# Common start addresses, and four small moves, in a transformer block with a dense mixture of 16,384 experts

## The chip, the cores and the metric

The kernel runs on one core of a Trainium2 chip. The metric is the device time of one execution in microseconds. Its engines are named as in the profile: PE (TensorE, matrix products), DVE (VectorE), ACT (ScalarE), POOL (GpSimd) and SP (SyncE, which only issues DMAs here). Each engine works through its own list of instructions in order and waits for other engines and for DMAs by semaphores. PEld is PE's load of the weight operand, which overlaps its products.

## The reference

One layer over 512 frames and 16 meta tokens of 2048 features, in float32. Two attentions share one input projection; a gate weighs each branch; then a mixture of single-neuron experts (PEER) is added.

```python
hn = _rmsnorm(h, norm_mix_g[l])
proj = hn @ w_in[l]
c_q, c_kv, k_rope, q_sb, k_sb, v_sb, gate_a, gate_b = jnp.split(proj, split_at, axis=-1)
...
y_a = _mla_attention(q_nope, q_rope, k_nope, k_rope, v_a, chunk_id).reshape(b, lp, A_WIDTH)
y_b = _stick_breaking_attention(...).reshape(b, lp, B_WIDTH)
merged = (jax.nn.sigmoid(gate_a) * (y_a @ w_branch_a[l])
          + jax.nn.sigmoid(gate_b) * (y_b @ w_branch_b[l]))
h = h + merged @ w_out[l]
h = h + _peer(_rmsnorm(h, norm_ffn_g[l]), peer_w_q[l], peer_sub_keys[l], peer_u[l], peer_v[l])
...
def block(xb):                       # in _peer, for 128 tokens
    q = (xb @ w_q).reshape(PEER_BLOCK, PEER_HEADS, 2, PEER_HALF)
    s = jnp.einsum('thcd,hcnd->thcn', q, sub_keys).astype(jnp.float32)
    s1, i1 = lax.top_k(s[:, :, 0], PEER_TOPK)
    s2, i2 = lax.top_k(s[:, :, 1], PEER_TOPK)
    ...
    g = jax.nn.softmax(top_s, axis=-1).reshape(PEER_BLOCK, -1)
    h = jnp.einsum('tkd,td->tk', u[idx], xb)
    act = (g * jax.nn.gelu(h.astype(jnp.float32), approximate=False)).astype(xb.dtype)
    return jnp.einsum('tk,tkd->td', act, v[idx])
```

## The kernel before

**Products in three parts.** Each float32 operand is split into a high part that PE's fast float32 form holds exactly and the remainder: `hi = round(x)`, `lo = x - hi`. `mm3` (L256) then makes three products for every pair of operands: lo weights by hi input (L257), hi by lo (L258), hi by hi (L259). A weight tile of 128x1024 is loaded by SP into `wr` (L239, from `front`, `ut` or `vb`), ACT writes its high part `wh` (L245), DVE the remainder `wl` (L246). `wh` and `wl` come from a ring of three buffers in the pool `weights`; in the v stage every fourth comes from a pool of its own, `weights_v`, and in the u stage two of five from the upper part of `hgh` and `hgl` (`Tail`, then named hgh and hgl as weights too).

**Stages,** by start in the profile. From 0: the input projections (`proj`, L340) with the moving input `xh`, `xl`, in pieces of 512 columns (frames) or of two times 264 (frames and meta tokens), and stick-breaking attention between them. From 815: multi-head latent attention, whose outputs lie in `yah`, `yal`. From 974: the branch products with `yh_b`, `yl_b` and `yah`, `yal`, whose gated sum is split into `mgh`, `mgl`. From 1154: the output projection with `mgh`, `mgl`. From 1332: the expert queries (16 blocks `hc` with `hgh`, `hgl`, 512 columns) and their scores, from which the top 16 keys are ranked. From 1549: u. For 336 of the 512 tokens all 16,384 experts are computed, as dense products of 336 columns, in 128 groups e of 128 experts with two weight tiles each; the other 176 tokens fetch the rows of their chosen experts by indirect DMAs on POOL (`row`) and multiply them on DVE (L1257). From 2536: v, with `vah`, `val` as the input (activations times gates of 4 groups, 336 columns each), 32 steps of 8 weight tiles; rows of v are added up on DVE into `xg` (L1265), dense sums into `acc` (L1443).

**Order.** A tile scheduler orders each engine's instructions by dependences and its own estimate of costs, not by their place in the text. A dependence added by hand (`follows`, L1286) makes an instruction stand behind the last `wl` split on DVE without any semaphore.

**The places that the change touches.**
- Start addresses. The pools of the left side lie behind the constants, a tile of 337 float32 columns per partition, which holds the two selection tables `sel_b` and `sel_c` too; pools of the right side are placed from the other end. `pad_y` (L817) is a tile that nothing uses.
- Copied norms. `rh_` holds each token's norm. For the 48 tokens handled in the groups of rows `BC`, DVE copies norms into `rr` (shown as tile sc, L1076), PE transposes them (L1074, L1077) and DVE copies the results out to `rcol` and `rcolb` (L1078, L1080). This stands at block `hc == 1`.
- Gates. Routing (`routing`, L1186) turns ranked keys into gates; `gates_of` (L1126) then spreads them over the 16,384 experts: DVE makes one-hot tiles of a pair of tokens (L1144), ACT scales them into `wos` (L1161, three buffers), PE multiplies (L1155) three steps later in the text. In the u stage `beside` runs one gate step per half of a group and one routing step per half at first, and three of four from e = 20.
- Gate weights `wt` are a tile of their own; `gw_all` holds the gates of each token and is stored by SP (L930) for the rows' tokens.
- Residual addition. In steps 3 to 14 of the v stage the residual of one of the 12 first feature blocks is loaded into the one buffer `hres` at tile 0 of the step and added to `acc` (L1421) at tile 6.

Of the kernel before, what the change touches and what calls it, by code (L numbers as in the profile page):

```python
# [23 lines left out]
P = 128  # L24
# [44 lines left out]
def _constants():  # L69
# [11 lines left out]
        "sel_b": (p[:, None] * NS[1] // P == np.arange(NS[1])[None, :]),  # L81
        "sel_c": (p[:, None] * NS[2] // P == np.arange(NS[2])[None, :]),
        "eps": np.full((P, 1), EPS),
        "halfpi": np.full((P, 1), math.pi / 2),
# [16 lines left out]
for _i in range(4):  # L101
    MLA_MASK[_i, META + P * _i + 64:META + P * (_i + 1)] = NEG
    MLA_MASK[_i, LEN + P * _i:LEN + P * _i + 64] = 1.0
GAINS = {"mix": (0, 16), "q": (16, 20), "kv": (20, 24), "ffn": (24, 40), "fin": (40, 56)}
# [26 lines left out]
def _layout(x, positions, meta_tokens, norm_mix_g, w_in, mla_q_norm_g, mla_w_uq, mla_kv_norm_g,  # L131
# [50 lines left out]
    for i, n in enumerate(FRONT):  # L182
# [10 lines left out]
            "pos": c(pos[None]), "gains": c(gains), "mla_mask": MLA_MASK, "const": CONST_ARR[0], "const_m": CONST_ARR[1], "const_e": CONST_ARR[2],  # L193
# [22 lines left out]
def body(tc, nc, a, dbg=None):  # L216
# [399 lines left out]
    yal = yp.tile([P, H, SEQ], F32R, name="yal")  # L616
    stage = ExitStack()
# [199 lines left out]
    sp2.tile([P, 16], F32, name="pad_y")  # L817
# [108 lines left out]
    def spread_rows():  # L926
        b0 = ND - (NT - 1) * P

        SP.dma_start(eob_d, er[b0:])
        SP.dma_start(gwb_d, gw_all[b0:, NT - 1])  # L930
        for o, t0, n in ((0, NS[2], NS[1]), (NS[1], 0, NS[2])):
            for to, src in ((eob, eob_d), (gwb, gwb_d)):
                SP.dma_start(to[:, o:o + n], src[t0:t0 + n].rearrange("t (r k) -> (t r) k", r=P // n))
# [4 lines left out]
    def route(ti, n, pool):  # L938
# [57 lines left out]
        if ti == NT - 1:  # L996
            V.tensor_copy(er, ev)

# [13 lines left out]
    with tc.tile_pool(name="score", bufs=2, side="left") as sp_, \  # L1012
# [28 lines left out]
        for hc in range(16):  # L1041
# [28 lines left out]
            if hc == 1:  # L1070
                pt_ = ps_tile()
                rr = sp_.tile([P, 4, NK], F32, name="sc")
                V.memset(rh_[:, :ND], 1.0)
# [44 lines left out]
    wos = up.tile([P, 3, 2, P, 2], F16, name="wos", bufs=1)  # L1118
    piece = up.tile([P, P], F16, name="piece", bufs=1)
    wt = up.tile([P, 2, P], F32, name="wt", bufs=1)  # L1120
# [5 lines left out]
    def gates_of(ti):  # L1126
# [8 lines left out]
        V.tensor_copy(wt[:, 0], piece)  # L1135
        V.scalar_tensor_tensor(rest, w, GW, wt[:, 0], ALU.mult, ALU.subtract)
        V.tensor_copy(piece, rest)
        V.tensor_copy(wt[:, 1], piece)
# [3 lines left out]
        for p in range(m + 4):  # L1142
            if p < m:
                V.tensor_tensor(ohs[p % 4], keys_b[:, :, None, 2 * p:2 * p + 2].to_broadcast([P, 2, P, 2]),  # L1144
                                iota_b[:, None].to_broadcast([P, 2, P, 2]), ALU.is_equal)
            yield
            gate_out()
            q0 = p - 3
            if q0 >= 0 and q0 % 2 == 0 and q0 < m:
                bank = ps_tile()  # L1150
                for q in range(q0, min(q0 + 2, m)):
                    for t in range(2):
                        o = ((q - q0) * 2 + t) * P
                        for c in (1, 0):
                            T.matmul(bank[:, o:o + P], ohs[q % 4][:, 1, :, t], wos[:, q % 3, c, :, t],  # L1155
                                     start=c == 1, stop=c == 0)
                banks.append((bank, ti * P + 2 * q0, min(4, n - 2 * q0)))
            if p < m:
                for t in range(2):
                    for c in range(2):  # L1160
                        after_gelu(S.activation(wos[:, p % 3, c, :, t], ohs[p % 4][:, 0, :, t], AF.Copy,  # L1161
                                                scale=wt[:, c, 2 * p + t:2 * p + t + 1]))
# [137 lines left out]
    for e in range(NK):  # L1300
# [7 lines left out]
        def beside(hf):  # L1308
# [3 lines left out]
            for _ in range(1 if e < 20 or e % 2 else hf):  # L1312
# [32 lines left out]
    ys.append(acc[:, :, TA:])  # L1345

# [44 lines left out]
    for i, step in enumerate(STEPS):  # L1391
        if i == NG - 1:
            assert gs["done"] == len(todo)
            ln_exp(more["last"])
            gather_sums(lambda c: xgb[:, c * P:(c + 1) * P], BC[1], C("sel_b"))
# [7 lines left out]
        for qi, (g, q8) in enumerate(step):  # L1403
# [10 lines left out]
            if (i, qi) == (20, 0):  # L1414
                assert gs["done"] > NU + NS[2]
                gather_sums(lambda c: acc[:, c, TA:], BC[0], C("sel_c"))
# [3 lines left out]
            if qi == 6 and 3 <= i < 15:  # L1420
                V.tensor_add(acc[:, i - 3, :ND], acc[:, i - 3, :ND], hres)  # L1421
# [51 lines left out]
```

## Time and profile before

| | |
|---|---|
| median of 3 runs | 3532.36 us (3526.85 to 3533.31) |
| profiled execution | 3537.0 us, of which the span of the trace is 3535.2 us |
| granted clock of the core | 0.995 |
| PE busy | 3488.5 us (99%), 21,097 products |
| DVE busy | 2569.1 us (73%) |
| ACT busy | 1430.6 us (40%) |
| POOL busy | 727.4 us (21%) |
| DMA | 901.03 MB, mean 255 GB/s |

The predicted time is compared with a median of runs; durations come from the one profiled execution. Products overlap in the records, so that a busy PE says little of its pace: the distance from one start to the next does. An instruction's row gives in brackets how long its engine stood idle before it, and what ended that.

### The profile page before, as it was taken

The page shows a single profiled execution, that of the slowest core. Times are in us where ns is not written, and L with a number is a line of the kernel's source. Part 1 is how long each engine was busy: PE and PEld are TensorE (multiplying, and loading weights), DVE is VectorE, ACT ScalarE, POOL GpSimd, SP SyncE. Part 2 cuts the span into 40 slices and gives each one's busy share as a digit, 9 for nine tenths or more (in the row PEclk, how much of TensorE's full clock was granted, in tenths as well). Part 3 has the DMA queues.
Part 4 walks back from the last instruction along what each step waited for, and adds up shares of the span by engine and source line. Part 5 has one row for each costly group of instructions (what it writes and reads, how often), then busy time and mean ns, then how long its engine had stood idle before and what let it go on. Part 6 is the DMA issues. An engine that isn't in the chain of part 4 may idle for free.

```text
span 3535.2 us, 53416 instructions
## 1 busy us (share of the span) xinstructions
PE 3488.5 (99%) x21097; PEld 3234.9 (92%) x21097; DVE 2569.1 (73%) x3545; ACT 1430.6 (40%) x2323; POOL 727.4 (21%) x539
## 2 busy tenths in 40 slices
PE   9999999999999999999999999999999999999997
PEld 8988888888888887899999999999999999999997
DVE  5533333435754557789999988887788989989987
ACT  4223223334543223233666666664333333333333
POOL 1000000000011122112232333322222423323320
PEclk9999999999999999999999999999999999999998
DMA  4322222222144344249999999999999999999993
GB/s 170 101 97 96 96 96 96 92 99 73 53 141 137 133 140 134 91 173 353 351 382 390 397 400 406 407 403 403 365 383 369 376 363 392 394 370 391 396 371 111
DMA packets 223964, 901.03 MB, mean 255 GB/s; under 512 B 27084, under 2 KB 52780, under 8 KB 178352
## 3 DMA queue, kind: packets, MB, share of 16 engines
q1 hardware_dynamic: 133792, 463.45, 36.2%
q0 software_dynamic: 58176, 394.96, 28.0%
q10 hardware_dynamic: 31744, 39.20, 3.1%
q8 instruction: 165, 2.70, 0.3%
q14 instruction: 87, 0.71, 0.1%
HBM read 835.21 MB, written 61.26 MB: 254 GB/s over the span
## 4 chain that ended last, share of the span: by engine, by line
PE 79%; DVE 12%; DMA 5%; issue 3%; ACT 1%; POOL 0%; SPq 0%; DVEq 0%; ACTq 0%; POOLq 0%
PE ps L257 25%; PE ps L258 25%; PE ps L259 25%; DVE wl L246 2%; DVE xg L1265 2%; DMA wr<-vb 2%; DVE row L1257 2%; DMA wr<-ut 1%; PE ps L1155 1%; DMA hres<-ht_d 1%; DVE hgl L246 1%; DVE acc L1265 1%; DVE acc L1443 0%; DVE val L263 0%; DMA row<-u,eo 0%
## 5 line engine op out<-in xcount | busy, mean ns | idle before, releaser
L245 ACT ACTIVATE wh<-wr 128x1024 fp32r<-128x1024 f32 (+1 forms) x654 | 688.4, 1054 | 1473.6 <-PE ps L259 1113.8
L246 DVE TENSOR_TENSOR wl<-wr,wh 128x1024 fp32r<-128x1024 f32 (+1 forms) x639 | 810.7, 1275 | 393.0 <-ACT wh L245 392.6
L257 PE MATMUL ps<-vah,wl 128*128 128x336 f32 x2048 | 651.6, 318 | 13.1 <-DVE wl L246 13.0
L259 PE MATMUL ps<-vah,wh 128*128 128x336 f32 x2048 | 649.8, 317 | 0.0
L258 PE MATMUL ps<-val,wh 128*128 128x336 f32 x2048 | 649.5, 317 | 0.0
L257 PE MATMUL ps<-hgh,wl 128*128 128x336 f32 (+1 forms) x1488 | 494.6, 332 | 0.7 <-DVE wl L246 0.7
L259 PE MATMUL ps<-hgh,wh 128*128 128x336 f32 (+1 forms) x1488 | 492.4, 331 | 0.0
L258 PE MATMUL ps<-hgl,wh 128*128 128x336 f32 (+1 forms) x1488 | 491.9, 331 | 0.0
L257 PE MATMUL ps<-xh,wl 128*128 128x512 f32 (+1 forms) x1376 | 472.0, 343 | 0.4 <-ACT xh L363 0.2
L259 PE MATMUL ps<-xh,wh 128*128 128x512 f32 (+1 forms) x1376 | 470.6, 342 | 0.0
L258 PE MATMUL ps<-xl,wh 128*128 128x512 f32 (+1 forms) x1376 | 470.1, 342 | 0.2 <-DVE xl L364 0.2
L257 PEld LDWEIGHTS ps<-vah,wl 128*128 128x128 f32 x2048 | 386.6, 189 | 16.8 <-DVE wl L246 16.4
L258 PEld LDWEIGHTS ps<-val,wh 128*128 128x128 f32 x2048 | 387.1, 189 | 0.0
L259 PEld LDWEIGHTS ps<-vah,wh 128*128 128x128 f32 x2048 | 385.7, 188 | 0.0
L1244 POOL DMA_INDIRECT row<-v,eo x128 | 227.6, 1778 | 488.6 <-DVE xg L1265 438.9
L1265 DVE SCALAR_TENSOR_TENSOR xg<-row,act,xg 128x2048 f32<-128x2048 f32 x127 | 298.1, 2347 | 2.1 <-DMA row<-v,eo 2.1
L1257 DVE SCALAR_TENSOR_TENSOR row<-row,xg 128x2048 f32<-128x2048 f32 x128 | 292.3, 2284 | 2.8 <-DMA row<-u,eo 2.7
L257 PEld LDWEIGHTS ps<-hgh,wl 128*128 128x128 f32 x1488 | 280.1, 188 | 12.5 <-DVE wl L246 1.2
L259 PEld LDWEIGHTS ps<-hgh,wh 128*128 128x128 f32 x1488 | 280.0, 188 | 11.9 <-issue 0.2
L258 PEld LDWEIGHTS ps<-hgl,wh 128*128 128x128 f32 x1488 | 280.3, 188 | 11.1
L257 PEld LDWEIGHTS ps<-xh,wl 128*128 128x128 f32 x1376 | 259.5, 189 | 33.4 <-ACT xh L363 1.8
L258 PEld LDWEIGHTS ps<-xl,wh 128*128 128x128 f32 x1376 | 259.1, 188 | 32.9 <-DVE xl L364 1.0
(500 smaller groups left out, 5934.4 us busy)
## 6 DMA issues: line engine op xcount, KB each, us to landing
wr<-ut SPq DMA_DIRECT2D x256, 512.0 KB, 9.4
wr<-vb SPq DMA_DIRECT2D x256, 512.0 KB, 7.4
wr<-front SPq DMA_DIRECT2D x238, 512.0 KB, 3.3
h_d<-hb ACTq DMA_DIRECT2D x128, 168.0 KB, 8.2
g_d<-gb POOLq DMA_DIRECT2D x42, 512.0 KB, 11.8
gin<-g_d SPq DMA_DIRECT2D x32, 672.0 KB, 8.4
hin<-h_d SPq DMA_DIRECT2D x32, 672.0 KB, 8.5
gates<-gt ACTq DMA_DIRECT2D x32, 256.0 KB, 2.0
```

What stands on the lines that cost most here:

```text
L245: more["last"] = S.activation(hi[:, s], r, AF.Copy)
L246: more["lo"] = (eng or V).tensor_sub(lo[:, s], r, hi[:, s].bitcast(F32))
L257: T.matmul(ps, wl, xh, start=start, stop=False)
L258: T.matmul(ps, wh, xl, start=False, stop=False)
L259: T.matmul(ps, wh, xh, start=False, stop=stop)
L1155: T.matmul(bank[:, o:o + P], ohs[q % 4][:, 1, :, t], wos[:, q % 3, c, :, t], start=c == 1, stop=c == 0)
L1244: G.indirect_dma_start(out=row, out_offset=None, in_=a[src], in_offset=bass.IndirectOffsetOnAxis(ap=eos[part][:, k:k + 1], axis=0))
L1257: ins = V.scalar_tensor_tensor(row, row, 1.0, xs[part], ALU.mult, ALU.mult, accum_out=w)
L1265: ins = V.scalar_tensor_tensor(y, row, w, y, ALU.mult, ALU.add)
```

## The change

**Start addresses.** The constants lose the two tables (48 columns) and gain 40 columns `pad`, so that everything on the left begins 32 bytes earlier per partition. The tables become an input of their own, `select`, loaded by one DMA in the v stage. On the right `pad_y` goes and `pad_ya` comes ahead of the attention's tiles. In the two built programs the starts, in bytes modulo 256, are:

| tile | before | after |
|---|---|---|
| weights wr, wh, wl | 192 | 160 |
| weights_v wh, wl | 64 | 32 |
| xh, xl, as 512 columns are read | 160 | 160 |
| xh, xl, the two pieces of 264 | 96, 128 | 96, 128 |
| yah, yal | 224 | 160 |
| yh_b, yl_b | 160 | 160 |
| mgh, mgl | 192 | 160 |
| hgh, hgl | 160 | 160 |
| vah, val (four groups) | 0, 64, 128, 192 | 224, 32, 96, 160 |
| row, hin, gin, gb | 0 | 224 |
| acc | 224 | 32 |

**Copied norms** are copied and turned at block 4 instead of block 1. **Gates:** in the text the products of pair p - 4 stand ahead of the one-hots of pair p, where those of p - 3 stood ahead of the `wos` of p, with four buffers of `wos`; routing runs at half the pace for the first 8 groups, at full pace up to 24 and three of four from there; `piece` and `wt` share other tiles, the high gate weights being written in place over `gw_all`; the two stores that precede are issued at the end of the last `route`. **Residual addition:** `follows` places it behind the last `wl` split of its time.


```diff
@@ -78,9 +78,8 @@
         "first": np.where(np.arange(TOPK) < 4, 16 * np.arange(TOPK), 48 + 4 * np.arange(TOPK))[None, :] * np.ones((P, 1)),
-        "sel_b": (p[:, None] * NS[1] // P == np.arange(NS[1])[None, :]),
-        "sel_c": (p[:, None] * NS[2] // P == np.arange(NS[2])[None, :]),
         "eps": np.full((P, 1), EPS),
+        "pad": np.zeros((P, 40)),
         "halfpi": np.full((P, 1), math.pi / 2),
@@ -101,6 +100,7 @@
     MLA_MASK[_i, LEN + P * _i:LEN + P * _i + 64] = 1.0
+SELECT = np.concatenate([np.arange(P)[:, None] * n // P == np.arange(n)[None, :] for n in NS[1:]], axis=1).astype(np.float32)
 GAINS = {"mix": (0, 16), "q": (16, 20), "kv": (20, 24), "ffn": (24, 40), "fin": (40, 56)}
@@ -614,6 +614,7 @@
     yal = yp.tile([P, H, SEQ], F32R, name="yal")
+    yp.tile([P, 16], F32, name="pad_ya")
     stage = ExitStack()
@@ -814,7 +815,6 @@
         ys.append((yh_, yl_))
-    sp2.tile([P, 16], F32, name="pad_y")
     mixer.close()
@@ -924,10 +924,6 @@
     def spread_rows():
-        b0 = ND - (NT - 1) * P
-
-        SP.dma_start(eob_d, er[b0:])
-        SP.dma_start(gwb_d, gw_all[b0:, NT - 1])
         for o, t0, n in ((0, NS[2], NS[1]), (NS[1], 0, NS[2])):
@@ -995,6 +991,9 @@
             V.tensor_copy(er, ev)
+            b0 = ND - (NT - 1) * P
+            SP.dma_start(eob_d, er[b0:])
+            SP.dma_start(gwb_d, gw_all[b0:, NT - 1])
 
@@ -1068,9 +1067,10 @@
             if hc == 1:
+                V.memset(rh_[:, :ND], 1.0)
+            if hc == 4:
                 pt_ = ps_tile()
                 rr = sp_.tile([P, 4, NK], F32, name="sc")
-                V.memset(rh_[:, :ND], 1.0)
                 T.transpose(pt_[:, :P], rh_[:, TA:], ident)
@@ -1115,9 +1115,9 @@
     ohs = [x[:, i] for x in (rh_.bitcast(F16).rearrange("p (i c k t) -> p i c k t", i=2, c=2, t=2), more_oh) for i in range(2)]
-    wos = up.tile([P, 3, 2, P, 2], F16, name="wos", bufs=1)
-    piece = up.tile([P, P], F16, name="piece", bufs=1)
-    wt = up.tile([P, 2, P], F32, name="wt", bufs=1)
+    wos = up.tile([P, 4, 2, P, 2], F16, name="wos", bufs=1)
+    piece = more_oh.rearrange("p i c k t -> p (i c k t)")[:, :P]
+    wt_low = up.tile([P, P], F32, name="wt_low", bufs=1)
 
@@ -1132,34 +1132,35 @@
         V.tensor_scalar(piece, w, GW, None, ALU.mult)
-        V.tensor_copy(wt[:, 0], piece)
-        V.scalar_tensor_tensor(rest, w, GW, wt[:, 0], ALU.mult, ALU.subtract)
+        wt = gw_all[:, ti], wt_low
+        V.tensor_copy(wt[0], piece)
+        V.scalar_tensor_tensor(rest, w, GW, wt[0], ALU.mult, ALU.subtract)
         V.tensor_copy(piece, rest)
-        V.tensor_copy(wt[:, 1], piece)
+        V.tensor_copy(wt[1], piece)
         yield
         n = min(P, ND - ti * P)
         m = n // 2
-        for p in range(m + 4):
-            if p < m:
-                V.tensor_tensor(ohs[p % 4], keys_b[:, :, None, 2 * p:2 * p + 2].to_broadcast([P, 2, P, 2]),
-                                iota_b[:, None].to_broadcast([P, 2, P, 2]), ALU.is_equal)
-            yield
-            gate_out()
-            q0 = p - 3
+        for p in range(m + 5):
+            q0 = p - 4
             if q0 >= 0 and q0 % 2 == 0 and q0 < m:
                 bank = ps_tile()
                 for q in range(q0, min(q0 + 2, m)):
                     for t in range(2):
                         o = ((q - q0) * 2 + t) * P
                         for c in (1, 0):
-                            T.matmul(bank[:, o:o + P], ohs[q % 4][:, 1, :, t], wos[:, q % 3, c, :, t],
+                            T.matmul(bank[:, o:o + P], ohs[q % 4][:, 1, :, t], wos[:, q % 4, c, :, t],
                                      start=c == 1, stop=c == 0)
                 banks.append((bank, ti * P + 2 * q0, min(4, n - 2 * q0)))
             if p < m:
+                V.tensor_tensor(ohs[p % 4], keys_b[:, :, None, 2 * p:2 * p + 2].to_broadcast([P, 2, P, 2]),
+                                iota_b[:, None].to_broadcast([P, 2, P, 2]), ALU.is_equal)
+            yield
+            gate_out()
+            if p < m:
                 for t in range(2):
                     for c in range(2):
-                        after_gelu(S.activation(wos[:, p % 3, c, :, t], ohs[p % 4][:, 0, :, t], AF.Copy,
-                                                scale=wt[:, c, 2 * p + t:2 * p + t + 1]))
+                        after_gelu(S.activation(wos[:, p % 4, c, :, t], ohs[p % 4][:, 0, :, t], AF.Copy,
+                                                scale=wt[c][:, 2 * p + t:2 * p + t + 1]))
 
@@ -1309,7 +1310,7 @@
                 rows_due(e)
-            for _ in range(1 if e < 20 or e % 2 else hf):
+            for _ in range(hf if e < 8 else 1 if e < 24 or e % 2 else hf):
                 if next(steps, steps) is steps and not gs["third"]:
@@ -1343,6 +1344,8 @@
     ys.append(acc[:, :, TA:])
+    select = ap2.tile([P, NB], F32, name="select")
+    SP.dma_start(select, a["select"])
 
@@ -1392,7 +1395,7 @@
             ln_exp(more["last"])
-            gather_sums(lambda c: xgb[:, c * P:(c + 1) * P], BC[1], C("sel_b"))
+            gather_sums(lambda c: xgb[:, c * P:(c + 1) * P], BC[1], select[:, :NS[1]])
             for c in range(0, KC, 4):
@@ -1413,12 +1416,12 @@
                 assert gs["done"] > NU + NS[2]
-                gather_sums(lambda c: acc[:, c, TA:], BC[0], C("sel_c"))
+                gather_sums(lambda c: acc[:, c, TA:], BC[0], select[:, NS[1]:])
             if qi in (0, 3) and 21 <= i < 29:
                 c = 2 * (i - 21) + qi // 3
                 residual(c, acc[:, c, TA:], slice(TA, SEQ))
             if qi == 6 and 3 <= i < 15:
-                V.tensor_add(acc[:, i - 3, :ND], acc[:, i - 3, :ND], hres)
+                follows(V.tensor_add(acc[:, i - 3, :ND], acc[:, i - 3, :ND], hres), "not before its load is due")
             if i + 1 < NG and qi == (QS if i else 4):
```

What this does to DVE's list around the copied norms, in the query stage. Before (qf, pql: a block's queries; sc: the copied norms, or scores; wl: the next weight tile's remainder):

```order
L1064 TENSOR_TENSOR qf<-ps,rh__9389 128x512
L1076 COPY sc<-rh__9389 128x128
L1073 MEMSET rh__9389 128x336
L1076 COPY sc<-rh__9389 128x128
L246 TENSOR_TENSOR wl<-wr,wh 128x1024
L263 TENSOR_TENSOR pql<-qf,pqh 128x512
L1078 COPY rcol<-ps 128x1
```

The two copies and the fill of `rh_` stand ahead of the split wl. After the change, at the same place:

```order
L1063 TENSOR_TENSOR qf<-ps,rh__9389 128x512
L246 TENSOR_TENSOR wl<-wr,wh 128x1024
L263 TENSOR_TENSOR pql<-qf,pqh 128x512
L1070 MEMSET rh__9389 128x336
L913 MAX lists<-sc 128x8 x2
```

The split follows qf at once. The copies are found three blocks later, behind that block's pql:

```order
L1063 TENSOR_TENSOR qf<-ps,rh__9389 128x512
L246 TENSOR_TENSOR wl<-wr,wh 128x1024
L263 TENSOR_TENSOR pql<-qf,pqh 128x512
L1076 COPY sc<-rh__9389 128x128 x2
L913 MAX lists<-sc 128x8 x2
L914 MAX_INDEX lists<-lists,sc 128x8
```

So they moved behind a split and the queries' remainder instead of ahead of them, and PE's transposes of them stand in the block behind this one.

DVE's list in the v stage, at the second and third of the twelve residual additions, before (val: the next step's remainder; xg: row sums):

```order
L1443 TENSOR_TENSOR acc<-acc,ps 128x336 x2
L263 TENSOR_TENSOR val<-hin,vah 128x1344
L246 TENSOR_TENSOR wl<-wr,wh 128x1024
L1421 TENSOR_TENSOR acc<-acc,hres 128x336
L246 TENSOR_TENSOR wl<-wr,wh 128x1024 x2
L1443 TENSOR_TENSOR acc<-acc,ps 128x336
L1421 TENSOR_TENSOR acc<-acc,hres 128x336
L1443 TENSOR_TENSOR acc<-acc,ps 128x336
L1265 SCALAR_TENSOR_TENSOR xg<-row,act,xg 128x2048
```

Between the second and the third addition, which belongs to the next step, stand only two splits and one sum. After the change, a stretch that ends a little behind the third one:

```order
L1266 SCALAR_TENSOR_TENSOR xg<-row,act,xg 128x2048
L1446 TENSOR_TENSOR acc<-acc,ps 128x336
L1293 TENSOR_TENSOR hin<-hin,gin 128x21x4x16
L1446 TENSOR_TENSOR acc<-acc,ps 128x336
L246 TENSOR_TENSOR wl<-wr,wh 128x1024 x2
L263 TENSOR_TENSOR val<-hin,vah 128x1344
L246 TENSOR_TENSOR wl<-wr,wh 128x1024
L1446 TENSOR_TENSOR acc<-acc,ps 128x336
L1424 TENSOR_TENSOR acc<-acc,hres 128x336
L1446 TENSOR_TENSOR acc<-acc,ps 128x336
L1266 SCALAR_TENSOR_TENSOR xg<-row,act,xg 128x2048
L246 TENSOR_TENSOR wl<-wr,wh 128x1024 x2
```

The third addition now stands two rows behind the next val and its split, as the second does in both kernels.

More of the change, by code (lines that the diff above doesn't have):

```diff
@@ L192, in _layout @@
     return {"front": front, "ut": c(ut), "vb": c(vb), "u": c(u), "v": c(v), "xt": c(xt),
-            "pos": c(pos[None]), "gains": c(gains), "mla_mask": MLA_MASK, "const": CONST_ARR[0], "const_m": CONST_ARR[1], "const_e": CONST_ARR[2],
+            "pos": c(pos[None]), "gains": c(gains), "mla_mask": MLA_MASK, "select": SELECT, "const": CONST_ARR[0], "const_m": CONST_ARR[1], "const_e": CONST_ARR[2],
             "iota": c(np.broadcast_to(np.arange(P, dtype=np.float32), (P, P)))}
```

## The prediction

> **What bounds the kernel now.** I read the stretches by stage first, then the chain of waits, then the spacing of TensorE's products, then what TensorE waits for.
>
> ```profile
> span 3535.2 us, 53416 instructions
> 0.00:815.00 815.00, 813.11 (x4613) 705.38 (x4614) 346.36 (x399) 259.73 (x296) 49.74 (x54) 1.00 0.32 105
> ...
> 975.00:1154.00 179.00, 179.00 (x772) 144.07 (x771) 88.04 (x88) 69.74 (x91) 19.33 (x15) 1.00 0.45 141
> 1154.00:1332.00 178.00, 178.00 (x797) 145.25 (x796) 94.14 (x93) 51.42 (x76) 37.60 (x31) 1.00 0.40 135
> ...
> 1549.00:2536.00 987.00, 983.07 (x6783) 971.87 (x6782) 873.55 (x1237) 571.69 (x1240) 282.77 (x229) 1.00 0.98 383
> 2536.00:3516.00 980.00, 966.85 (x6235) 962.86 (x6234) 872.97 (x754) 320.38 (x318) 282.54 (x165) 0.99 0.92 359
> ```
>
> (The columns are the stretch, its length, busy time and instructions of each engine, the granted clock, the DMA engines' share, GB/s.) PE is busy nearly throughout: 813.11 of 815 us in the projections, 179.00 of 179.00 in the branch merge, 966.85 of 980 where it is least busy. The clock is granted in full. The early stages use 0.32 to 0.45 of the DMA engines' time; the two expert stages (1549 to 2536 for u, 2536 to 3516 for v) use 0.98 and 0.92.
>
> ```profile
> PE 79%; DVE 12%; DMA 5%; issue 3%; ACT 1%; POOL 0%; SPq 0%; DVEq 0%; ACTq 0%; POOLq 0%
> ```
>
> Followed back from the end, the chain stands on PE for 79%. So an edit shortens the span only if it shortens the spacing of products or one of PE's few gaps; inside the expert stages a shorter gap may also run into DMAs.
>
> Records of neighbouring products overlap, so the price of one is the distance between starts. Four pairs of rows from undisturbed stretches (start, duration; in between lie products of the same kind, 29, 17, 20 and 23 steps):
>
> ```profile
> 113.04 0.40 PE L257 MATMUL ps<-xh,wl 128*128 128x512 f32 x1
> ...
> 119.80 0.40 PE L259 MATMUL ps<-xh,wh 128*128 128x512 f32 x1
> 1139.73 0.40 PE L257 MATMUL ps<-yh_b,wl 128*128 128x512 f32 x1
> ...
> 1143.70 0.40 PE L259 MATMUL ps<-yh_b,wh 128*128 128x512 f32 x1
> 1385.06 0.40 PE L257 MATMUL ps<-hgh,wl 128*128 128x512 f32 x1
> ...
> 1389.73 0.40 PE L259 MATMUL ps<-hgh,wh 128*128 128x512 f32 x1
> 1193.84 0.39 PE L257 MATMUL ps<-mgh,wl 128*128 128x512 f32 x1
> ...
> 1199.06 0.39 PE L259 MATMUL ps<-mgh,wh 128*128 128x512 f32 x1
> ```
>
> 6.76/29 = 233 ns for the input xh, 3.97/17 = 233.5 for branch b, 4.67/20 = 233.5 for hgh, but 5.22/23 = 227 ns for the merged input mgh. All are 128x512 products with weights from the same ring of tiles. What differs is where the moving tile begins: in the program before, the weights begin at 192 bytes modulo 256 and so does mgh, while the other inputs begin at 160 or 224. Modulo 64 mgh agrees with its weights; the others lie 32 off. After the change the weights and all four inputs, as these products read them, begin at 160.
>
> **The change part by part. Addresses.** How many products it concerns, by groups:
>
> ```profile
> L257 PE MATMUL ps<-xh,wl 128*128 128x512 f32 x704 | 280.2, 398 | 0.4 <-ACT xh L363 0.2
> L257 PE MATMUL ps<-hgh,wl 128*128 128x512 f32 x256 | 103.4, 404 | 0.7 <-DVE wl L246 0.7
> L257 PE MATMUL ps<-mgh,wl 128*128 128x512 f32 x256 | 102.1, 399 | 0.0
> L257 PE MATMUL ps<-yh_b,wl 128*128 128x512 f32 x128 | 50.6, 396 | 0.0
> L257 PE MATMUL ps<-yah,wl 128*128 128x512 f32 x128 | 50.6, 395 | 0.0
> ```
>
> Each group has two sisters (L258, L259) of equal count. 3 x 704 = 2112 xh products at 233.1 - 227.0 = 6.1 ns are 12.9 us; 3 x (128 + 128) = 768 branch products at 6.5 are 5.0; 3 x 256 = 768 hgh products at 6.5 are 5.0. Together **23 us** off, if equal places are the cause; mgh stays at 227. Bounds: 0 (places are not the cause), or 5.0 us lost if what counts is a moving start at a multiple of 64, which mgh gives up (768 x 6.5 ns). Nothing else hides in these stages: PE is busy for 179.00 of 179.00 us in the branch merge. I take 23, since four groups sort by their place and nothing else I see sorts them.
>
> The narrower products need their own rows:
>
> ```profile
> 2214.11 0.32 PE L257 MATMUL ps<-hgh,hgl 128*128 128x336 f32 x1
> ...
> 2217.63 0.32 PE L259 MATMUL ps<-hgh 128*128 128x336 f32 x1
> 2219.09 0.32 PE L259 MATMUL ps<-hgh,wh 128*128 128x336 f32 x1
> ...
> 2225.53 0.32 PE L259 MATMUL ps<-hgh,wh 128*128 128x336 f32 x1
> 2650.33 0.31 PE L257 MATMUL ps<-vah,wl 128*128 128x336 f32 x1
> ...
> 2661.90 0.32 PE L257 MATMUL ps<-vah,wl 128*128 128x336 f32 x1
> 108.19 0.29 PE L259 MATMUL ps<-xh,wh 128*128 128x264 f32 x1
> ...
> 111.10 0.29 PE L259 MATMUL ps<-xh,wh 128*128 128x264 f32 x1
> ```
>
> 336 columns with hgl/hgh as weights (160 against 160, equal): 3.52/23 = 153.0 ns. The same input with wl/wh (160 against 192, 32 off): 6.44/42 = 153.3. The v products (places equal modulo 64, before and after): 11.57/75 = 154.3. So I cost the 9840 products of 336 columns at nothing (at most 3696 x 0.3 = 1 us off). Of the 264-column products of xh one half begins at 96, one at 128, in turn; modulo 64 the first was off and becomes equal, the second the reverse. Their mixed spacing is 2.91/24 = 121 ns. One half should lose what the other gains, so I take 0, with 1008 x 6.6 ns = 6.7 us on either side (the halves are 2016/2).
>
> The Trainium skill, page "TensorE: Matmul & The Clock Gate", Part 2, step 1, says that the streaming operand and the weight load have two independent read ports and that the load takes no bandwidth from a running product. By that rule no place relative to the weights could matter and this term would be 0. The page's gap of 512/2.4 + about 2.5 ns is 216 ns; the trace has 227 and 233, so the trace does not follow its figure, and something outside the rule separates mgh.
>
> **Copied norms.** They move from query block 1 to block 4.
>
> ```profile
> 1360.21 1.77 DVE L1076 COPY sc<-rh__9389 128x128 f32<-128x128 f32 x1
> 1362.34 1.21 DVE L246 TENSOR_TENSOR wl<-wr,wh 128x1024 fp32r<-128x1024 f32 x1
> 1362.04 0.91 PE L1077 MATMUL ps<-cst,sc 128*128 128x128 f32 x2 [3.46 <-DVE sc L1076]
> 1363.60 0.80 PE L257 MATMUL ps<-hgh,wl 128*128 128x512 f32 x1 [0.65 <-DVE wl L246]
> ```
>
> (First column start, second duration; brackets hold the idle time and what ended it.) PE waits 3.46 us for the copied column sc, then 0.65 for wl. On DVE the copies, from 1360.21 on, stand ahead of that wl, which ends at 1363.55 (1362.34 + 1.21). Without them wl starts at 1360.2 and ends near 1361.4: **2.1 us** earlier, and PE's next product waits for it alone. In the new order the copies stand on DVE in block 3, its transposes on PE in block 4, a block of 48 products x 233 ns = 11 us later, so no wait follows them; uncovered, they would cost the 3.46 again. What the transposes make, rcol and rcolb, is first read by ScalarE at 2252.9. Bounds 0 to 4.1 (3.46 + 0.65).
>
> **Gate products a step later.**
>
> ```profile
> L1155 PE MATMUL ps<-wos,more_oh x336: 217/218/233, 1710.9 to 2415.8; 128*128 128x128 f16 x168
> ...
>   PE ps L1155: 3.0, 7
> ```
>
> PE waits 3.0 us in 7 places for ScalarE's wos, 0.4 us each (the first row gives the spans of single products and the first and last start). The text makes the products a step later and gives wos a fourth buffer. In the engines' lists little of this is seen: counted in weight tiles, a pair of the first token block has its one-hots on DVE, its wos on ScalarE and its products on PE eight or nine tiles later (pair 4: splits 275 to 284, 292 to 300, product tiles 47 to 55), so their distances stay; only in the second and third block do some wos move a tile ahead of their products, and no wait of 0.2 us is found there. ScalarE did not wait for PE to free wos, so the fourth buffer takes no wait away. The slower start of the routing spares DVE, whose lateness makes wos late, in the first groups, but the load behind is the same. I take **1 us**; bounds 4 (by the starts around these waits) and -3, the present waits once more, since all of it meets other transfers at a DMA share of 0.98. POOL's stores of the gates and SP's loads of them move too: 4 to 5 groups, 5 x 987/128 = 39 us, behind the last gate product at 2415.8, which leaves 80 us to the end of the stage.
>
> **Residual addition pinned.**
>
> ```profile
> DVE acc L1421 <- DMA hres<-ht_d: 19.5, 4, 5.6
> 2772.24 0.65 PE L257 MATMUL ps<-vah,wl 128*128 128x336 f32 x1 [3.00 <-DVE wl L246]
> hres<-ht_d ACTq DMA_DIRECT2D x12, 168.0 KB, 8.1
> L257 PE MATMUL ps<-vah,wl 128*128 128x336 f32 x2048 | 651.6, 318 | 13.1 <-DVE wl L246 13.0
> ```
>
> The twelve additions hold DVE idle for 19.5 us in four waits for hres (in us, times, longest): the scheduler had put some of them ahead of their loads' landing. Behind such an addition stand xg and wl on DVE; the late wl reaches PE, as at 2772.24 (3.00 us). PE's waits for wl are 13.0 us in the v stage. One, of 1.9 near 2555.7, comes ahead of the first addition. Of the other 11 I take 8: DVE is busy for 873 of 980 us there, so some backlog forms without the waits too, and the DMA share is 0.92. Bounds 4 and 11. In the new order each addition is behind the last wl of its own tile, one per step and no longer in pairs, six tiles after its load was issued: 980 us for 256 tiles make 3.8 a tile, 23 us against a landing of 8.1. The pin adds a wait between instructions of DVE itself, so nothing new queues up. Its load, on ScalarE's queue, must wait for the addition before it to free the one hres buffer; that has some 7 us of slack.
>
> **Edits at no cost.** The select table is one small load on SP in the v stage, many tiles ahead of its use; uncovered it would be one landing. The gate weights wt are now written in place over gw_all, so the cast must wait for the store that reads it. The store is issued at 1637.1, the first cast starts at 1696.6; without these 59 us it would wait for one landing. The landings (last column) of rows and weight tiles:
>
> ```profile
> row<-u,eo POOLq DMA_INDIRECT x128, 11.3
> wr<-vb SPq DMA_DIRECT2D x256, 512.0 KB, 7.4
> ```
>
> Row tiles, hin and gin move from 0 to 224 modulo 256. Rows land in 11.3 us today; the weight tiles wr, which begin off a multiple of 256 already, land in 7.4 with 512 KB. I see no sign that an off start is dear, and take 0; for more, see the fourth rival.
>
> **Sum:** 23 + 2.1 + 1 + 8 = 34 us. The profiled execution took 3537.0 us (span 3535.2 and 1.8 around it), 4.6 above the median 3532.4 of the runs shown. Against itself the sum gives 3503; against the median **3498 us**.
>
> **Rivals.** First, half of the spacing comes back (230 ns): places matter, but 160 is not as good as 192. 3498 + 11.5 = 3510. Nothing speaks for it but that equal places at 32 past a multiple of 64 are not in the trace with 512 columns; against it, the 336-column products at 160/160 lose nothing.
>
> Second, places don't matter and mgh is quick for another reason, such as less other traffic in its stage: only the 11 us of waits go, 3532.4 - 11.1 = 3521. Against it: the branch merge just ahead has the same DMA share (0.45 against 0.40) and runs at 233.5. This is also the time by the Trainium skill's rule of two ports.
>
> Third, not the relation but the moving tile's own start at a multiple of 64 counts, for 512 columns. Then mgh loses 5.0 and no other gains: 3526. For it: mgh is the only 512-wide input at such a start, so the trace cannot part it from my forecast. Against it: the v products have such starts and are no quicker than the u products at 160.
>
> Fourth, rows and gate tiles at 224 make DMAs longer. The Trainium skill's page "DMA: Bandwidth & Descriptors", section "How a descriptor splits into AXI transactions", says that a descriptor off a 256-byte boundary fetches beats that it does not use; for 8 KB rows I estimate 263 instead of 256 beats, 2.7%, from that page; no row here parts the two. From rows alone: the u stage uses 0.98 of the DMA time, so 20 us of its 987 are free; if each of its 128 row loads takes a quarter of a us more of its 11.3, that is 32 us, 12 more than are free: 3510.
>
> Fifth, on the other side, **slower**: the own start counts for 336 columns too, and v's quick starts (0, 64, 128, 192) become 224 + 64j, 32 past a multiple of 64. All 6144 v products then lose up to 6.5 ns, 40 us, and mgh 5.0, against 11.1 gained: 3566. It makes the kernel slower from (11.1 - 5.0)/6144 = 1.0 ns a product on. Against it: u at 160 runs at 153.3, v at 154.3, so the start that v would lose buys nothing today.
>
> **How the numbers follow.** Forecast 0.61, half 0.08, nothing from places 0.09, own start for 512 0.13, longer DMAs 0.04, v slower 0.05. The forecast's own range is 3485 to 3510: upward, 264-column products lose 6.7, gates 4 and the addition 4, not all at once; downward, 264 gains 6.7, norms 2, gates 3, addition 3, likewise. For 8 in 10 the range takes in the second rival and about half of the third: 3482 to 3526. A measurement of this kernel tells 0.2%, 7 us, from no change, so faster means under 3525.3. Faster: 0.60 of the forecast, 0.08, 0.07 of the second, 0.05 of the third, 0.03 of the fourth = 0.83; same, what is left of these: 0.12; slower, the fifth: 0.05.
>
> **What would show it.** Starts of xh, branch and hgh products 227 ns apart, mgh's unchanged: the first step; 233 with mgh at 233: the third rival; 233 with mgh at 227: the second. PE's wait for sc gone, its waits for wos about as before. The group of the pinned addition without idle time before it and the v stage's wait for wl at 5 us or less. v products still 154 ns apart. The forecast is wrong if the spacing stays, or if wr or row waits take the place of those removed.

## The result and the profile after

| | before | after |
|---|---|---|
| median of 4 runs each | 3531.05 us (3526.85 to 3533.31) | 3496.05 us (3493.95 to 3497.62) |
| profiled execution | 3537.0 us | 3495.88 us |
| span of the trace | 3535.2 us | 3494.1 us |

The ratio is 0.9902, with a 95% interval of 0.9885 to 0.9919: 35 us off, between 29 and 41. The forecast was 3498.

The head of the page after and its chain of waits, which stood on PE for 79% before:

```profile
span 3494.1 us, 53314 instructions
...
PE 93%; DVE 4%; DMA 2%; issue 1%; ACT 0%; POOL 0%; SPq 0%; DVEq 0%; ACTq 0%; POOLq 0%
```

The chain now runs through PE almost alone; DVE's 12% and the DMAs' 5% have shrunk to 4% and 2%.

The two traces side by side, by the start of each stage's first product:

| stage | before, us | after, us | change | prediction's terms |
|---|---|---|---|---|
| projections | 816.1 | 803.3 | -12.8 | -12.9 |
| latent attention | 159.3 | 161.5 | +2.2 | 0 |
| branch products | 179.7 | 175.3 | -4.4 | -5.0 |
| output projection | 178.2 | 178.7 | +0.5 | 0 |
| queries | 208.4 | 202.9 | -5.5 | -5.0 and -2.1 |
| u | 995.6 | 990.4 | -5.2 | -1 |
| v | 978.7 | 963.4 | -15.3 | -8 |
| end | 19.2 | 18.6 | -0.6 | 0 |

Together -41.1 us, against -34 forecast; the profiled execution of before was 6 us above the median, that of after was at it, so the traces differ by more than the medians. Latent attention takes 159 to 163 us in the traces below, whatever their edit, so its +2.2 is not put down to the change.

The spacing of the 512-column products, after, in the order xh, branch b, hgh, mgh (34, 23, 35 and 19 steps from the first row of a pair to the second):

```profile
112.08 0.40 PE L257 MATMUL ps<-xh,wl 128*128 128x512 f32 x1
...
119.79 0.39 PE L258 MATMUL ps<-xl,wh 128*128 128x512 f32 x1
1123.80 0.39 PE L257 MATMUL ps<-yh_b,wl 128*128 128x512 f32 x1
...
1129.01 0.39 PE L259 MATMUL ps<-yh_b,wh 128*128 128x512 f32 x1
1364.80 0.39 PE L257 MATMUL ps<-hgh,wl 128*128 128x512 f32 x1
...
1372.74 0.39 PE L259 MATMUL ps<-hgh,wh 128*128 128x512 f32 x1
1179.78 0.39 PE L258 MATMUL ps<-mgl,wh 128*128 128x512 f32 x1
...
1184.08 0.40 PE L259 MATMUL ps<-mgh,wh 128*128 128x512 f32 x1
```

7.71/34 = 226.8 ns, 5.21/23 = 226.5, 7.94/35 = 226.9 and 4.30/19 = 226.3: all four are now where only mgh was. xh begins at 160 in both kernels; its weights alone have moved. The v products, 86 steps:

```profile
2629.72 0.32 PE L259 MATMUL ps<-vah,wh 128*128 128x336 f32 x1
...
2643.00 0.31 PE L258 MATMUL ps<-val,wh 128*128 128x336 f32 x1
```

13.28/86 = 154.4 ns against 154.3: unchanged, as the prediction had it. The 264-column products of xh went from 121.1 to 121.7 ns on the mean of neighbours, 1.1 us on 2016 of them. What the v stage lost are waits, the group of its first products first, then all of PE's waits for a split wl on DVE (us in total, times, longest):

```profile
L257 PE MATMUL ps<-vah,wl 128*128 128x336 f32 x2048 | 648.9, 317 | 3.3 <-DVE wl L246 3.3
```

```profile
PE ps L257 <- DVE wl L246: 8.0, 5, 4.2
```

The page's 13.0 us of waits for wl in v have become 3.3, and DVE waits for hres no more. Of the 8.0 us that are left in the whole kernel 4.2 are one wait, in the query stage, at the place of the copied norms. The rows of that place, of POOL, DVE and PE:

```profile
1342.46 4.06 POOL L246 TENSOR_TENSOR wl<-wr,wh 128x1024 fp32r<-128x1024 f32 x1 [10.70 <-ACT wh L245]
1344.23 0.68 DVE L1063 TENSOR_TENSOR qf<-ps,rh__9389 128x512 f32<-128x512 f32 x1
1344.83 2.77 DVE L246 TENSOR_TENSOR wl<-wr,wh 128x1024 fp32r<-128x1024 f32 x1
1347.66 0.79 PE L257 MATMUL ps<-hgh,wl 128*128 128x512 f32 x1 [4.15 <-DVE wl L246]
```

The copies are gone from DVE's list, the split wl follows qf at once, and yet it ends at 1347.60 and PE waits 4.15 us: the split takes 2.77 us instead of 1.2.

### The profile page after: what moved, and what is told of

Same layout as the page of the kernel before. It is cut to its first block, busy times and chain, and to the rows that moved or that the text cites. A ratio compares the mean times of both kernels' runs of the same rounds, so it can differ in the third digit from the quotient of the medians.

```text
span 3494.1 us, 53314 instructions
## 1 busy us (share of the span) xinstructions
PE 3461.7 (99%) x21097; PEld 3233.3 (93%) x21097; DVE 2572.3 (74%) x3545; ACT 1429.4 (41%) x2323; POOL 728.9 (21%) x539
## 4 chain that ended last, share of the span: by engine, by line
PE 93%; DVE 4%; DMA 2%; issue 1%; ACT 0%; POOL 0%; SPq 0%; DVEq 0%; ACTq 0%; POOLq 0%
PE ps L257 30%; PE ps L258 29%; PE ps L259 29%; PE ps L1151 1%; DVE wl L246 1%; DMA wr<-ut 1%; DMA row<-u,eo 0%; PE ps L769 0%; DMA row<-v,eob 0%; DVE xn L1059 0%; PE ps L491 0%; DVE acc L1382 0%; PE ps L778 0%; PE ps L1355 0%; DVE acc L1266 0%
## 5 line engine op out<-in xcount | busy, mean ns | idle before, releaser
L1245 POOL DMA_INDIRECT row<-v,eo x128 | 209.7, 1638 | 480.5 <-DVE xg L1266 442.3
```

Of the source, the lines that this page charges most:

```text
L1245: G.indirect_dma_start(out=row, out_offset=None, in_=a[src], in_offset=bass.IndirectOffsetOnAxis(ap=eos[part][:, k:k + 1], axis=0))
```

## The experiments

All are edits of the changed kernel. Medians are compared with its 3496.05 us; runs of one kernel lie within 3 to 11 us of each other, so that 2 us between medians say little, and the rows of the trace say more. The changed kernel was not run again beside the experiments, but the kernel before was. Its medians there are 3528.54 us (beside the moved weights and the split of POOL), 3528.22 (beside pin, pace, gates and norms) and 3527.39 (beside the two kernels with several edits), 2.5 to 3.7 less than the 3531.05 of the result. So a difference from 3496.05 is uncertain by some 3 us; where that matters, the distance from the kernel before of the same set is given too, which for the changed kernel was 35.0.

**Weights moved against their inputs.** Three widths of the constants; the order of every engine's list stays. The edit of the first, and of the third:

```diff
-        "pad": np.zeros((P, 40)),
+        "pad": np.zeros((P, 48)),
```

> The changed kernel with the constants 8 columns (32 bytes) wider: weights, mgh, row and gate tiles begin where they did before (192, 192, 0), xh, y and hgh stay at 160; the order of every engine is that of the changed kernel. Theory A (products of 512 columns are quick when moving tile and weights begin at the same place): xh, yh_b, yah and hgh back to 233 ns, mgh stays at 227, 3648 products x 6.4 ns = 23 us more, near 3519 us. Rival (the gain of the changed kernel came from the moved instructions, and the starts only go along): spacing 227 and 3496 us.

Measured: 3519.34 us. xh (34 steps):

```profile
112.86 0.40 PE L257 MATMUL ps<-xh,wl 128*128 128x512 f32 x1
...
120.78 0.40 PE L258 MATMUL ps<-xl,wh 128*128 128x512 f32 x1
```

7.92/34 = 232.9 ns; mgh, still equal to its weights at 192, stays at 227. 3648 products times the 6.4 ns between the kernels are 23.3 us, and 3519.34 - 3496.05 is 23.3. That the two agree to a tenth is chance: the kernel is 9.2 us faster than the kernel before of its set, 25.8 less than the changed kernel's 35.0. The addresses do it, not the moved instructions.

The second (pad of 8 columns, weights at 32):

> Constants 128 bytes narrower: weights and mgh at 32, xh, y and hgh at 160. They agree modulo 128, and not modulo 256. Theory A64 or A128 (agreement modulo 64 or 128 is enough): all 512-column products at 227 ns, about 3496 us. Rival A256 (agreement modulo 256 is needed): xh, y and hgh at 233, mgh at 227, about 3519 us.

Measured: 3517.47 us. xh (26 steps):

```profile
114.81 0.39 PE L257 MATMUL ps<-xh,wl 128*128 128x512 f32 x1
...
120.84 0.40 PE L259 MATMUL ps<-xh,wh 128*128 128x512 f32 x1
```

6.03/26 = 231.9 ns, though 160 and 32 agree modulo 128; mgh, at 32 like its weights, keeps a median distance of 227. The theory of modulo 64, on which the prediction leaned in words, falls, and that of modulo 128 with it.

```diff
-        "pad": np.zeros((P, 40)),
+        "pad": np.zeros((P, 24)),
...
-    yp.tile([P, 16], F32, name="pad_ya")
```

> Constants 64 bytes narrower and no pad ahead of the attention tiles: weights and mgh at 96, xh and hgh at 160 (agree modulo 64 only), yah and yh_b at 224 (agree modulo 128). Theory A64: all at 227 ns, about 3496 us. A128: yah, yh_b and mgh at 227, xh and hgh at 233, 2880 x 6.4 = 18 us more, about 3514. A256: only mgh at 227, about 3519.

Measured: 3506.14 us, which none of the three had. xh at 64 past its weights (110 steps), and branch b at 128 past (23 steps):

```profile
149.68 0.39 PE L257 MATMUL ps<-xh,wl 128*128 128x512 f32 x1
...
174.85 0.39 PE L259 MATMUL ps<-xh,wh 128*128 128x512 f32 x1
1133.34 0.39 PE L257 MATMUL ps<-yh_b,wl 128*128 128x512 f32 x1
...
1138.68 0.40 PE L259 MATMUL ps<-yh_b,wh 128*128 128x512 f32 x1
```

25.17/110 = 228.8 ns for 64 and 5.34/23 = 232.2 for 128. Over all neighbours in the traces, xh and y, the mean distance by the place of the input past the weights, modulo 256, is:

| bytes past | 0 | 32 | 64 | 128 | 224 |
|---|---|---|---|---|---|
| ns | 226.9 | 233.4 | 229.1 | 232.5 | 233.3 |
| seen in | after | before (yah) | weights at 96 | weights at 32 and 96 | before (xh, yh_b) |

So the price is graded: none at the same place, a third of it at 64, nearly all at 32, 128 and 224. With 229.1 for xh and hgh and 232.5 for y one gets 2880 x 2.2 + 768 x 5.6 = 10.6 us; measured are 10.1, or 12.6 by the kernel before of the set.

**The pin undone.**

```diff
-                follows(V.tensor_add(acc[:, i - 3, :ND], acc[:, i - 3, :ND], hres), "not before its load is due")
+                V.tensor_add(acc[:, i - 3, :ND], acc[:, i - 3, :ND], hres)
```

> The changed kernel without the pin: the residual additions stand again in pairs, at the places of the kernel before. Theory (the prediction's term): DVE waits for hres again, some 20 us in four to six waits, PE waits for wl in the v stage rise from 3 to about 13 us, and the time by 8 us to 3504. Rival 1: each of these PE waits is followed by a dozen products at half the clock, which the prediction left out, so the pin is worth the whole 15 us by which the v stage shrank in the profiles: 3511. Rival 2: the v stage of the profiled execution of before was a dear one, and in most runs DVE's waits are covered: 3496 to 3500.

Measured: 3508.59 us, 12.5 more. DVE's waits for hres and PE's waits for wl in this kernel:

```profile
DVE acc L1424 <- DMA hres<-ht_d: 19.9, 4, 6.0
```

```profile
PE ps L257 <- DVE wl L246: 19.3, 14, 4.8
```

All 19.9 us of DVE's waits are back, and PE's waits for wl are 19.3 us instead of 8.0 (in v 14.5 instead of 3.3); the v stage takes 979.5 us in the trace, 16 more. The time lies between the theory's 3504 and rival 1's 3511, nearer to rival 1 (by the kernel before of the set the pin is worth 15.4); rival 2 falls. But rival 1's reason isn't there. Behind the longest wait of v in this trace:

```profile
2746.75 0.42 PE L257 MATMUL ps<-vah,wl 128*128 128x336 f32 x1 [2.52 <-DVE wl L246]
2747.00 0.32 PE L258 MATMUL ps<-val,wh 128*128 128x336 f32 x1
2747.16 0.32 PE L259 MATMUL ps<-vah,wh 128*128 128x336 f32 x1
```

One product takes 0.25 us, the next come 0.155 apart as always; none of the nine waits of v over 0.5 us is followed by a dozen slow products.

**Gates and pace, one at a time and together.**

```diff
-            for _ in range(hf if e < 8 else 1 if e < 24 or e % 2 else hf):
+            for _ in range(1 if e < 20 or e % 2 else hf):
```

> The changed kernel with the routing pace of before (full pace up to group 20); gate products as changed. Theory (the prediction's step: it is the spared DVE, not the order of the products, that takes PE's waits for wos away): those waits of 3 to 4 us return, near 3500 us. Rival (the fourth wos buffer and the products behind wos do it): no wait for wos, 3496 us.

Measured: 3497.91 us, and no wait for wos on PE. One wait for wl of 4.28 us, ahead of the product at 2533.45, some 20 us into v, is new. The theory that the spared DVE does it falls, as far as the waits for wos go.

For the next, the loop of `gates_of` as in the kernel before, with three buffers of `wos`:

> The changed kernel with the gate loop of before (products ahead of the wos of the same step, three buffers); routing pace as changed. Theory (the pace does it): no wait for wos on PE, 3496 us. Rival (the gate loop does it): PE waits for wos 3 to 4 us, near 3500.

Measured: 3496.17 us, with PE's wait for wos:

```profile
PE ps L1156 <- ACT wos L1162: 1.2, 2, 0.9
```

1.2 us in two places, of 3.0 in seven before. Each of the two edits alone takes most of these waits away. Both undone at once, and with them the pin and the place of the norms:

> The changed kernel with the pin, the gate loop, the routing pace and the norms of before, so that of the change mainly the addresses are left. Theory (gates, pace and norms together are worth no more than about 2 us beside the pin's 12): 3508 to 3511. Rival (they hide behind each other: the waits for wos return only when loop and pace are both undone, as the u stage's 5 us less in the profiles says): PE waits for wos some 3 us, u stage near 995 us, 3512 to 3515.

Measured: 3511.70 us. PE's wait for wos:

```profile
PE ps L1155 <- ACT wos L1161: 2.1, 5, 0.9
```

2.1 us in five places, and the u stage takes 992.5 us against 990.4: more than with either alone, less than the rival's 3 us and 995. Against the kernel without the pin it is 3.1 us slower, which covers gates, pace and norms, and lies close to the spread of the runs. Against the kernel before of its own set it is only 15.7 us faster (by the interval of the ratio, 13 to 23).

**The norms at block 1 again.**

```diff
             if hc == 1:
-                V.memset(rh_[:, :ND], 1.0)
-            if hc == 4:
                 pt_ = ps_tile()
                 rr = sp_.tile([P, 4, NK], F32, name="sc")
+                V.memset(rh_[:, :ND], 1.0)
```

> The changed kernel with the copied norms at block 1 again. Theory of the prediction: PE waits for sc and wl in block 1 as before, 2.1 us more, near 3498. Rival (as the profile of the changed kernel has it): DVE is held by POOL's split there either way, the move is worth 0.4 us, 3496.5.

Measured: 3494.03 us, 2.0 less (0.8 more by the kernel before of the set). PE waits 3.4 us for sc instead of 4.15 for wl; the query stage takes 203.9 us in the trace against 202.9. In the runs the move gains nothing that can be told.

**The split of POOL given to DVE.**

```diff
-                wh, wl = wq.pop((hc, hf)) if (hc, hf) in wq else front("wq", hc, hf, G if hf else V)
+                wh, wl = wq.pop((hc, hf)) if (hc, hf) in wq else front("wq", hc, hf, G if hf and hc != 2 else V)
```

> The second weight tile of query block 2 is split by DVE instead of POOL; nothing else moves. In the changed kernel the split of that block's first tile on DVE takes 2.77 us instead of 1.2 and ends 1.1 us behind POOL's split of the second (1342.46 to 1346.52). Theory: DVE's split is held until POOL's instruction ends; without POOL's it takes 1.2 and PE's wait of 4.2 us falls to about 2.6, some 2 us off with the slow restart, about 3494. Rival: DVE's split is slow for another reason (its operands, ScalarE's writes), stays at 2.8, and the wait stays at 4.2.

Measured: 3494.62 us. DVE's split and PE's wait:

```profile
1344.67 1.20 DVE L246 TENSOR_TENSOR wl<-wr,wh 128x1024 fp32r<-128x1024 f32 x1
1345.93 0.80 PE L257 MATMUL ps<-hgh,wl 128*128 128x512 f32 x1 [2.49 <-DVE wl L246]
```

The split takes 1.20 us and the wait falls to 2.49; the query stage takes 200.6 us instead of 202.9. The theory holds in the trace; in the medians 1.4 us is too little to tell, and by the kernel before of the set it is 1.1 us more, not less.

**This split, and cqh at the place of its weights.**

```diff
     kt = lp.tile([P, LEN], F32R, name="kt")
+    lp.tile([P, 48], F32, name="pad_cq")
```

> The changed kernel with the split of query block 2 on DVE, and the attention tiles 192 bytes further, so that cqh and cql too begin at 160 like their weights. Theory A256 (equal places modulo 256 make any 512-column product quick): cqh by wh and cql by wh fall from 233 to 227 ns, 144 products x 6 = 0.9 us; with the 2 us of the split about 3493. Rival (only the inputs of the long runs behave so): cqh stays at 231 to 235, 3494.6.

Measured: 3497.10 us, no gain. cql by wh falls from a mean of 233.1 to 228.6 ns, cqh by wh from 232.7 to 230.5, thus part of the way, in a stage where they come a few at a time between other products. Their mean over all three parts goes from 233.2 to 229.8 ns. In the other built programs these inputs lie at other places, with traces of 232.9 ns at 224 bytes past their weights (before), 233.2 at 192 (after) and 233.6 at 160 (weights at 192), but 229.8 and 229.7 at 64 (weights at 32 and 96). So they too lose little at 64 bytes, and here nothing at all against equal places. The 2 us of the split do not show in this kernel's runs either, so that no version tried is shown to beat the changed kernel.

## Why the prediction was right, by its steps

**Addresses, 23 us.** The term came out: 23.3 us by the medians with the weights moved back, 21 by the stages of the traces (12.8 + 4.4 - 0.5, and 4.5 of the queries' 5.5). The likeliest case was right, but its reason was stated too loosely: agreement modulo 64 was read from one input, mgh, which agreed with its weights modulo 256 too. The runs with weights at 32 and 96 show that 64 or 128 is not enough. Had the change put weights and inputs 128 bytes apart, the same words would have forecast a gain that is not there. The rivals fall: "nothing from places" and "the input's own start", by xh, which did not move and went from 233 to 227; "half of the spacing", by distances of 226.3 to 226.9 ns where it had 230. The Trainium skill's two independent read ports ("TensorE: Matmul & The Clock Gate", Part 2, step 1), by which, as the prediction read it, the place relative to the weights could not matter, do not fit these traces: 6.4 ns of 233 hang on that place.

**336 and 264 columns at nothing.** Right but for 1.1 us that the 264-column products lost. v's 154.4 ns speak against the input's own start alone: its inputs moved together with their weights, so that their places past them stayed 0, 64, 128 and 192. For the place past the weights u speaks: hgh went from 224 bytes past wl and wh to none, and these products from 153.39 to 153.41 ns on the mean. The slower rival falls with v. So does that of longer DMAs: DVE waits 1.8 us for rows of v, 2.1 before, and with the rows at 0 again (weights at 192) u and v are no shorter, 991.6 and 964.6 us against 990.4 and 963.7.

**Copied norms, 2.1 us: the size was off.** The step read the copy's 1.77 us as its cost. Two more rows of the kernel before, POOL's split of a weight tile and the copy's twin:

```profile
1357.83 4.07 POOL L246 TENSOR_TENSOR wl<-wr,wh 128x1024 fp32r<-128x1024 f32 x1 [11.38 <-ACT wh L245]
1362.26 0.16 DVE L1076 COPY sc<-rh__9389 128x128 f32<-128x128 f32 x1
```

The twin took 0.16; the rest of the 1.77 was a wait for POOL, whose split ended at 1361.90, the copy at 1361.98. With the copies gone the next instruction, wl, met the same POOL split and was held 1.6 us instead. The move is worth 1.0 us in the traces, none in the runs. The experiment without POOL's split showed this for the split wl; for the copy it is read off the rows, twice: with the norms at block 1 again the copy took 1.78 us and ended 0.09 us behind POOL's split.

**Gates, 1 us.** PE's waits for wos went altogether, 3.0 us by the page, and the u stage is 5.2 us shorter in the trace. The prediction found the lists to keep their distances and so expected the waits to stay; the runs show that either the slower pace or the later products take most of them away. Why the u stage shrank by 2 more than the waits is open; the kernel with gates and pace of before but the new addresses took 992.5 us there, so that by its one trace 3.1 of the 5.2 do not come from gates and pace.

**Residual addition, 8 us: the mechanism was right, the size off.** 12.5 us by the medians, 15 to 16 in the traces of v. The cut from 11 to 8, for a backlog that would remain, was not needed: of 13.0 us of waits for wl in v only 3.3 remain. Without the pin these waits are 14.5 us, 11.2 more than with it; by the distances between starts they cost 13.0 more, and products elsewhere in v that came over 200 ns behind the one before cost 3.2 more, for a reason that is open. One wait of the kernel before cost far more than its idle time. Its rows, behind the wait of 3.00 us at 2772.24 (start, duration), and the stretch that holds them (the last three figures are the granted clock, the DMA share and GB/s):

```profile
2772.69 0.48 PE L258 MATMUL ps<-val,wh 128*128 128x336 f32 x1
2772.97 0.48 PE L259 MATMUL ps<-vah,wh 128*128 128x336 f32 x1
...
2775.21 0.45 PE L258 MATMUL ps<-val,wh 128*128 128x336 f32 x1
2775.49 0.33 PE L259 MATMUL ps<-vah,wh 128*128 128x336 f32 x1
2775.65 0.31 PE L257 MATMUL ps<-vah,wl 128*128 128x336 f32 x1
```

```profile
2772.20:2775.00 2.80, 2.76 (x10) 2.76 (x11) 2.80 (x3) 1.06 (x1) 0.80 (x1) 0.50 1.00 420
```

At a granted clock of 0.50 the products come 280 ns apart up to 2775.49, then 155: eleven products at 126 ns too much are 1.4 us on top of the 3.0. The Trainium skill ("TensorE: Matmul & The Clock Gate", Part 1, "Wait — 56ns, not 53.3ns?") gives N / 1.2 GHz for the cold array; for 336 columns I estimate 280 ns from that, and the trace agrees. But the other waits of v in this trace, 0.9 to 1.8 us, were each followed by one slow product, 0.1 us, and those of the kernel without the pin by one or two. So the clock is not what made the pin worth more than 8.

By the medians the pin was taken 4.5 us too small and the norms 2 too dear; the two part errors have opposite signs, and beside a main term of the right size the sum came to 34 against 35. That it came so close is partly luck. One at a time the parts make 23.3 for the addresses, 12.5 for the pin and 3.1 for the rest, 38.9 us, 4 more than the whole. And the kernel with mainly the addresses has the quick products (xh at 226.8 ns) but is 15.7 us faster than the kernel before of its set, where 23 were forecast for them. Where the difference goes is open: the one trace of the kernel before, at 3537.0 us, is slower than all of its 36 other runs (3524.0 to 3536.6), and does not show where these are quicker.

## What to carry to other kernels

Take TensorE's pace from the distance between starts, and sort equal shapes by where their operands lie: a difference of 3% on a sixth of the products (3648 of 21,097) was worth more here than all the idle time of PE that went (30.0 us before, 16.6 after, in the traces). Before a duration is costed, compare it with its twins: a copy that takes 1.77 us where another takes 0.16 is a wait for somebody, and whatever takes its place will wait too. Take what a wait of TensorE costs from start to start as well: most cost little beyond their idle time, the few with a lower clock behind them half as much again. And when parts are measured one at a time, add them up: here they come to more than the whole.

## What the runs showed of the hardware

A 512-column float32 product by fresh weights took, in the long runs of xh and y, 226.9 ns where both operands began at the same place modulo 256 bytes, 229 at 64 bytes past it, 232.5 to 233.4 at 32, 128 and 224; the few of latent attention took 229.8 at the same place and at 64. 336 columns took 153 to 154 whatever the places, 264 columns 121.1 to 122.2. No run shows why, nor why 512 columns feel it and 336 do not.

In the queries and v, over all traces, PE's waits of 2.60 us and more were followed by six or more products at about half pace (427 ns for 512 columns, 280 for 336), waits of 1.4 to 1.8 us by one or two. In between, one of 2.49 us was followed by seven, one of 2.52 by one.

DVE's split wl, which reads two tiles of SBUF, ended 1.08 us behind the end of POOL's split (1342.46 + 4.06 = 1346.52, and 1347.60), about as long as it takes alone (1.20); DVE's qf, which reads one tile there and PSUM, was not held; in the kernel before a copy from one tile of SBUF to another was (1.77 us against 0.16). POOL's own split took 4.06 us there and 2.4 in 14 other places; in its first 1.8 us DVE was running splits of two tiles of SBUF one behind the other. That is what the Trainium skill says ("SBUF — State Buffer", "SBUF: two separate sides"): DVE and POOL share a pair of ports, whoever starts first holds it for a whole instruction, and DVE needs it where both inputs lie in SBUF or in a mode of two ports. The traces agree for two inputs; whether the copy ran in such a mode they do not show.
